# A two-layer recurrent and attention trunk: weight splits by halves, one copy of the small vectors, a later broadcast, and an earlier root table

## The chip, the cores and the metric

The kernel runs on one core of one Trainium2 chip. The metric is the device time of one execution in microseconds (us); of several runs the median is given. TensorE (PE in the profile, PEld for its weight loads) multiplies, VectorE (DVE), ScalarE (ACT) and GpSimd (POOL) work element by element, and SyncE (SP) issues nearly all DMA transfers. Each engine works through its own list of instructions in order and waits on semaphores where an instruction needs another engine's or a DMA's result.

## The reference

The input x has 1024 rows of 1024 numbers, in float32. Two layers follow each other; each has a token mixer and a feed-forward block, both with a residual add and an RMS norm ahead of them, and a last RMS norm ends the program. This is what is computed, cut to what matters here:

```python
def rms_norm(x, g):
    return x * lax.rsqrt(jnp.mean(x * x, axis=-1, keepdims=True) + 1e-6) * g

for layer in range(2):
    hn = rms_norm(h, mix_norm[layer])
    mixed = rg_lru_block(hn, ...) if layer == 0 else stick_breaking_attention(hn, ...)
    h = h + mixed
    h = h + swiglu_ffn(rms_norm(h, ffn_norm[layer]), ffn_w_in[layer], ffn_w_out[layer])
return rms_norm(h, final_norm)
```

The mixer of layer 0 projects the normed input to a recurrent branch and a gate branch (`lru_w_in`), runs a causal convolution of width 4 over the recurrent branch, forms two gates with block-diagonal weights (`lru_gate_w`), and scans `h = a * h + b` over the rows, where `a` depends on a softplus of `lru_lambda`. That of layer 1 is an attention with 16 heads of 64.

## The kernel before

**Tiling.** Activations are kept transposed, as `[d][n]` tiles of 128 features by 512 rows (n is 0 or 1). To keep float32 accuracy, each operand of a product is split into a rounded part and a rest (`xh` and `xl`, `whi` and `wlo`), and `mm3` (L140) issues three matmuls for each pair: L141 whi with xh, L142 whi with xl, L143 wlo with xh. A weight tile of 1024 x 128 is loaded as `raw`, ACT casts it to `whi` (L120), and POOL subtracts for `wlo` (L124). `raw` has three buffers; `whi` and `wlo` come from a ring of six, so a new weight pair waits until the matmuls have read the pair three before it.

**First phase (L251 to L359).** The order on every engine is the written one. SP loads x in eight parts, two weight tiles and nine small vectors (into `vraw`, L285). `group(n, d)` (L298) transposes four blocks on TensorE; ACT writes `xh` (L304), DVE writes a copy `hc` (L308) that SP stores to DRAM (L310), and then `xl` (L309). `project` (L247) makes 24 matmuls for one column tile and one half n. `square_rows` (L312) sums squares on ACT; `row_factors` (L316) turns them into the norm's factors through `rstd` (L174); `broadcast_r` (L185) spreads the factors over all partitions, with four transposes into PSUM on TensorE and a copy to `rbc[n]` on DVE (L196). The norm's factor is applied after the product: `stage_a` multiplies the result by `rbc[n]` (L444). At the end of this phase the broadcast of the second half's factors stands between the first and the second half of the last 24 matmuls (L357 to L359). The small vectors are transposed to columns `vc` at L345, with a matmul that waits for all of `vraw`'s transfers itself.

**Second phase (L362 to L518).** Only TensorE keeps the written order; the other engines' instructions are ordered by the framework's scheduler. A chain of some 45 tiny DVE instructions (L371 to L405) works out the softplus and the convolution's bias from `vc`: seven of them are L379, followed by L382 to L385. Then column tiles are projected, convolved (L446, L448), gated and scanned, in the order "A0 A1 B0 A2 G0 A3 ...". A0 and A1 use the two results of the first phase; B0 is the first projection of the gate branch, with PSUM from a pool (`psB`, L364) that takes over the banks of the first phase's pool `sps`. G0 needs the first gate weights, `rawg` (L415), which pass through the same cast and subtraction (L120, L124).

**The middle** is the two feed-forward blocks (seven products in place of eight by a Strassen-like scheme) and the attention; none of its lines is edited, except that `rstd` is used there too.

**The end (`finish`, L1215).** The last two feature tiles are finished in pieces: all four blocks of rows of n = 0, blocks 0 and 1 of n = 1, and blocks 2 and 3 of n = 1. `last` (L1220) makes the product, adds it to the residual (L1230), squares it (L1231), adds to the sum of squares (L1232) and applies the gain. `stats` (L198) sums over features by TensorE, and `rstd` makes the factors: a root on ACT (L178) and five small DVE instructions (L179 to L183). `turn` (L1235) transposes back (L1244), scales each block by its factor on ACT (L1246, odd blocks) or DVE (L1248), and SP stores it (L1249).

Of the kernel before, what the change touches and what calls it, by code (L numbers as in the profile page):

```python
# [8 lines left out]
F32 = mybir.dt.float32  # L9
F32R = mybir.dt.float32r  # L10
# [3 lines left out]
ALU = mybir.AluOpType  # L14
PSUM = bass.MemoryType.PSUM

P = 128
S = 1024
D = 1024
ND = D // P  # L20
# [13 lines left out]
def trunk(  # L34
# [22 lines left out]
    nc = tc.nc  # L57
    f32 = lambda t: t.bitcast(F32)
# [29 lines left out]
    wpool = [ring]  # L88


    ident = cp.tile([P, P], F32, name="ident")
    make_identity(nc, ident)
    ones = cp.tile([P, 1], F32, name="ones")
    nc.gpsimd.memset(ones, 1.0)
    vc = cp.tile([P, P], F32, name="vc")
# [11 lines left out]
    rcol = cp.tile([P, NT], F32, name="rcol")  # L107
# [9 lines left out]
    def split(raw, pool=None, tag="w", bufs=None, lo_eng=None, parts=1):  # L117
        pool = pool or wpool[0]
        hi = pool.tile([P, D], F32R, tag=tag, name="whi", bufs=bufs)
        nc.scalar.copy(hi, raw)  # L120
        lo = pool.tile([P, D], F32R, tag=tag, name="wlo", bufs=bufs)
        for i in range(parts):
            c = slice(i * D // parts, (i + 1) * D // parts)
            (lo_eng or nc.gpsimd).tensor_sub(lo[:, c], raw[:, c], f32(hi)[:, c])  # L124
        return hi, lo
# [48 lines left out]
    def rstd(dst, ms):  # L174
        n = dst.shape[-1]
        sq = cp.tile([P, max(n, 4)], F32, tag="rs_s", name="rs_s", bufs=2)[:, 0:n]
        t = cp.tile([P, max(n, 4)], F32, tag="rs_t", name="rs_t", bufs=2)[:, 0:n]
        nc.scalar.sqrt(sq, ms)  # L178
        nc.vector.reciprocal(sq, sq)  # L179
        nc.vector.tensor_mul(t, sq, sq)  # L180
        nc.vector.tensor_mul(t, t, ms)
        nc.vector.tensor_scalar(t, t, -0.5, 1.5, op0=ALU.mult, op1=ALU.add)
        nc.vector.tensor_mul(dst, sq, t)  # L183

    def broadcast_r(ps_pool, tag, n):  # L185
        ps = ps_pool.tile([P, NB], F32, tag=tag, name="rb_ps")
# [55 lines left out]
    half = lambda t, n: t[:, n * NB : (n + 1) * NB]  # L242
# [4 lines left out]
    def project(ps, w, n, ks=range(ND)):  # L247
        for k in ks:
            mm3(half(ps, n), w[0][:, k], w[1][:, k], xh[k][n], xl[k][n], k == 0, k == ND - 1)

    with ExitStack() as st, tc.manual_schedule(engines={E.PE, E.Activation, E.DVE, E.Pool, E.SP}):  # L251
        sp = st.enter_context(tc.tile_pool(name="sp", bufs=1))
        sps = st.enter_context(tc.tile_pool(name="sps", bufs=4, space=PSUM))
        vraw = sp.tile([P, P], F32, name="vraw")
        vmix = sp.tile([P, P], F32, name="vmix")
        g0 = sp.tile([P, ND], F32, name="g0")
        nc.scalar.dma_start(vmix[0:ND, :], mix_norm[0:1].rearrange("a (b c) -> (a b) c", c=P))
        xt = [sp.tile([P, 4, D], F32, name=f"xt{n}") for n in range(NH)]
        aw = []

        def load_x(n, g):
            cs = slice(g * 2 * P, (g + 1) * 2 * P)
            nc.sync.dma_start(
                xt[n][:, :, cs], x[0, n * NB : (n + 1) * NB, cs].rearrange("(i p) c -> p i c", p=P)
            )

        for g in range(3):
            load_x(0, g)
        aw.append(load_raw(cols(w_in, D), (ND,)))
        load_x(0, 3)  # L270
        aw.append(load_raw(cols(w_in, D + P), (ND,)))
        load_x(1, 0)
        load_x(1, 1)
        for base, src in (
            (V_MIX, mix_norm.rearrange("a (b c) -> (a b) c", c=P)),
            (V_FFN, ffn_norm.rearrange("a (b c) -> (a b) c", c=P)),
            (V_FIN, final_norm.rearrange("(b c) -> b c", c=P)),
            (V_BIN, lru_b_in.rearrange("a (b c) -> (a b) c", c=P)),
            (V_CW, lru_conv_w.rearrange("a k (b c) -> (a k b) c", c=P)),
            (V_CB, lru_conv_b.rearrange("a (b c) -> (a b) c", c=P)),  # L280
            (V_GB, lru_gate_b.rearrange("a g (b c) -> (a g b) c", c=P)),
            (V_LAM, lru_lambda.rearrange("a (b c) -> (a b) c", c=P)),
            (V_BO, lru_b_out.rearrange("a (b c) -> (a b) c", c=P)),
        ):
            nc.sync.dma_start(vraw[base : base + src.shape[0], :], src)  # L285
        load_x(1, 2)
        load_x(1, 3)
        ssum = sp.tile([P, NT], F32, name="ssum")
        ms = sp.tile([P, NT], F32, name="ms0")
        junk = sp.tile([P, D], F32, name="junk")  # L290
        pst = lambda name: sps.tile([P, NB], F32, tag="tp", name=name)
        k3 = lambda t: t.rearrange("p (k c) -> p k c", k=ND)

        ps = pst("vps0")
        nc.tensor.transpose(ps[:, 0:ND], vmix[0:ND, :], ident[0:ND, 0:ND])
        nc.vector.tensor_copy(g0, ps[:, 0:ND])

        def group(n, d):  # L298
            ps = pst("tp")
            for i in range(4):  # L300
                nc.tensor.transpose(ps[:, i * P : (i + 1) * P], xt[n][:, i, d * P : (d + 1) * P], ident)
            hc = sp.tile([P, NB], F32, tag="hc", name="hc", bufs=8)
            g = g0[:, d : d + 1]
            nc.scalar.activation(xh[d][n], ps, AF.Copy, scale=g)  # L304
            if d % 4 == 3:
                nc.scalar.copy(hc, ps)
            else:
                nc.vector.tensor_copy(hc, ps)  # L308
            nc.vector.scalar_tensor_tensor(xl[d][n], ps, g, f32(xh[d][n]), op0=ALU.mult, op1=ALU.subtract)  # L309
            nc.sync.dma_start(hd[d][n], hc)  # L310

        def square_rows(n, i):  # L312
            b = 4 * n + i
            nc.scalar.activation(junk, xt[n][:, i, :], AF.Square, accum_out=ssum[:, b : b + 1])

        def row_factors(n):  # L316
            nn = slice(4 * n, 4 * n + 4)
            nc.vector.tensor_scalar(ms[:, nn], ssum[:, nn], 1.0 / D, EPS, op0=ALU.mult, op1=ALU.add)
            rstd(rcol[:, nn], ms[:, nn])

        def wsplit(i):
            hi, lo = split(aw[i])
            aw[i] = (k3(hi), k3(lo))

        pa = [psl[0].tile([P, S], F32, tag="a", name="a_ps") for _ in range(2)]
        for d in range(6):
            group(0, d)
        wsplit(0)
        for d in (6, 7):
            group(0, d)  # L330
        wsplit(1)
        for i in range(4):
            square_rows(0, i)
        project(pa[0], aw[0], 0)
        group(1, 0)
        group(1, 1)
        row_factors(0)
        project(pa[1], aw[1], 0, range(4))
        group(1, 2)
        group(1, 3)  # L340
        project(pa[1], aw[1], 0, range(4, ND))
        group(1, 4)
        group(1, 5)
        ps = pst("vps")
        nc.tensor.transpose(ps[:, 0:P], vraw, ident)  # L345
        nc.vector.tensor_copy(vc, ps[:, 0:P])
        square_rows(1, 0)
        square_rows(1, 1)
        project(pa[0], aw[0], 1, range(4))
        group(1, 6)  # L350
        group(1, 7)
        square_rows(1, 2)
        square_rows(1, 3)
        broadcast_r(sps, "tp", 0)
        project(pa[0], aw[0], 1, range(4, ND))
        row_factors(1)
        project(pa[1], aw[1], 1, range(4))  # L357
        broadcast_r(sps, "tp", 1)
        project(pa[1], aw[1], 1, range(4, ND))  # L359


    with ExitStack() as st:  # L362
# [45 lines left out]
        ys = [lp.tile([P, S], F32, name=f"y{e}") for e in range(ND)]  # L408
# [188 lines left out]
    def mix_out_ffn_in(h, mix, bias, layer, gnext, ob):  # L597
# [124 lines left out]
        with tc.manual_schedule(engines={E.PE, E.Activation, E.DVE, E.Pool}):  # L722
# [484 lines left out]
            if final:  # L1207
                finish(h, nw, R, pp, (*GT, *UT))
# [6 lines left out]
    def finish(h, w, R, pp, rows):  # L1215
        ys = {}
# [18 lines left out]
        def turn(n, i0, i1, hf):  # L1235
            cs = slice(hf * NB, (hf + 1) * NB)
            for i in range(i0, i1):
                b = 4 * n + i
                if hf == 0:
                    ys[b] = rp.tile([P, D], F32, tag="raw", name="y") if b < 3 else rows[b - 3]  # L1240
                ps = pp.tile([P, NB], F32, tag="p", name="e_ps")
                for j in (1, 2, 3, 0):
                    d = 4 * hf + j
                    nc.tensor.transpose(ps[:, j * P : (j + 1) * P], h[d][n][:, i * P : (i + 1) * P], ident)  # L1244
                if i % 2:
                    nc.scalar.activation(ys[b][:, cs], ps, AF.Copy, scale=rcol[:, b : b + 1])  # L1246
                else:
                    nc.vector.tensor_scalar_mul(ys[b][:, cs], ps, rcol[:, b : b + 1])  # L1248
                nc.sync.dma_start(out[0, b * P : (b + 1) * P, cs], ys[b][:, cs])  # L1249

        first, mid, end = (0, 0, 4), (1, 0, 2), (1, 2, 4)
        for piece in (first, mid):
            for x in range(2):
# [39 lines left out]
    with ExitStack() as st:  # L1293
# [249 lines left out]
        with tc.manual_schedule(engines={E.PE, E.Activation, E.DVE, E.Pool, E.SP}):  # L1543
# [20 lines left out]
            c = 0  # L1564
# [69 lines left out]
```

## Time and profile before

| | us |
|---|---|
| median of 3 runs | 2195.74 |
| lowest and highest of them | 2195.57 and 2196.19 |
| time of the profiled execution | 2195.37 |
| its span, first to last instruction | 2193.6 |
| TensorE busy in the span | 2167.9 |
| VectorE busy | 1711.4 |
| ScalarE busy | 1155.4 |
| GpSimd busy | 315.7 |

In the profile's rows a line of the timeline has the start in us from the start of the span, the duration in us, the engine, the line of the kernel, the operation, output and inputs with shapes, a count where equal instructions follow each other, and in brackets how long the engine had been idle before it and what ended that. A row of the waits has the engine and line that waited, what it waited for, the us in total, how many times, and the longest.

### The profile page before, as it was taken

What the parts mean: (1) busy time and instruction counts of PE and PEld (TensorE: products, weight loads), DVE (VectorE), ACT (ScalarE), POOL (GpSimd) and SP (SyncE); (2) the same over time, 40 slices, a digit from 0 to 9 for tenths busy, and PEclk for the clock granted to TensorE, in tenths of its full rate; (3) what the DMA queues carried; (4) which work ended last, traced back from release to release, by engine and by line L of the source; (5) the groups of instructions that cost most, each with busy time, mean ns of one, the idle gap of its engine ahead of it and who ended that gap; (6) DMA issues with size and microseconds to landing.
All of it is one profiled execution on the core that took longest, in us unless ns stands there. A gap on an engine that the chain in (4) does not pass through costs nothing.

```text
span 2193.6 us, 28494 instructions
## 1 busy us (share of the span) xinstructions
PE 2167.9 (99%) x10120; PEld 1803.3 (82%) x10120; DVE 1711.4 (78%) x2383; ACT 1155.4 (53%) x2031; POOL 315.7 (14%) x443
## 2 busy tenths in 40 slices
PE   8999999999999999999999999999999999999998
PEld 6888888888888888888888888878888888888887
DVE  6887778667777887887888888876876777788886
ACT  5567435334444544556666666753543444454556
POOL 2222020000000000004444444531000000000002
PEclk9999999999999999999999999999999999999999
DMA  7111412334444764434333333551133444467442
GB/s 232 49 48 39 135 39 64 110 125 152 141 145 138 250 221 129 148 117 104 89 106 90 94 98 105 173 169 54 48 115 116 149 146 143 144 228 236 137 153 87
DMA packets 297677, 277.71 MB, mean 127 GB/s; under 512 B 15288, under 2 KB 214080, under 8 KB 297536
## 3 DMA queue, kind: packets, MB, share of 16 engines
q1 hardware_dynamic: 297520, 275.90, 40.6%
q8 instruction: 79, 1.29, 0.2%
q14 instruction: 62, 0.51, 0.1%
q10 hardware_dynamic: 16, 0.00, 0.0%
HBM read 175.71 MB, written 74.97 MB: 114 GB/s over the span
## 4 chain that ended last, share of the span: by engine, by line
PE 95%; DVE 2%; ACT 1%; DMA 1%; SPq 0%; issue 0%; DVEq 0%; ACTq 0%
PE p_ps L143 18%; PE p_ps L141 18%; PE p_ps L142 18%; PE qk_ps L143 4%; PE qk_ps L141 4%; PE qk_ps L142 4%; PE wt_ps L1465 3%; PE ob_ps L141 2%; PE ob_ps L142 2%; PE ob_ps L143 2%; PE a_ps L141 2%; PE a_ps L142 2%; PE a_ps L143 2%; PE z_ps L1427 2%; PE z_ps L1428 2%; PE av_ps L1487 2%
## 5 line engine op out<-in xcount | busy, mean ns | idle before, releaser
L1452 POOL TENSOR_TENSOR w<-w,F 128x128 f32<-128x128 f32 (+1 forms) x192 | 192.5, 1002 | 268.3 <-DVE F L1449 164.6
L141 PE MATMUL p_ps<-vh,wch 128*128 128x512 f32 x524 | 204.2, 390 | 0.0
L143 PE MATMUL p_ps<-vh,wal 128*128 128x512 f32 x524 | 204.1, 389 | 0.1
L143 PE MATMUL p_ps<-vh,wbl 128*128 128x512 f32 x524 | 204.1, 390 | 0.0
L143 PE MATMUL p_ps<-vh,wcl 128*128 128x512 f32 x524 | 204.1, 390 | 0.0
L141 PE MATMUL p_ps<-vh,wbh 128*128 128x512 f32 x524 | 204.1, 390 | 0.0
L142 PE MATMUL p_ps<-vl,wch 128*128 128x512 f32 x524 | 203.9, 389 | 0.0
L142 PE MATMUL p_ps<-vl,wbh 128*128 128x512 f32 x524 | 203.9, 389 | 0.0
L141 PE MATMUL p_ps<-vh,wah 128*128 128x512 f32 x524 | 203.9, 389 | 0.0
L142 PE MATMUL p_ps<-vl,wah 128*128 128x512 f32 x524 | 203.8, 389 | 0.0
L668 ACT CAST wbh<-sb 128x1024 fp32r<-128x1024 f32 (+2 forms) x69 | 69.6, 1009 | 193.1 <-DVE sb L652 193.1
L1474 ACT CAST th<-wt_ps 128x512 fp32r<-128x512 f32 x192 | 92.6, 482 | 126.3 <-PE wt_ps L1465 125.8
L212 POOL TENSOR_TENSOR acc<-acc,rbc 128x512 f32<-128x512 f32 x30 | 41.6, 1386 | 771.9 <-ACT rbc L211 771.9
L1475 DVE TENSOR_TENSOR tl<-wt_ps,th 128x512 fp32r<-128x512 f32 x192 | 105.6, 550 | 48.9 <-ACT th L1474 46.9
L141 PE MATMUL qk_ps<-vh,whi 128*128 128x512 f32 x264 | 118.1, 447 | 0.0
L1449 DVE TENSOR_TENSOR_SCAN F<-F,unit 128x128 f32<-128x128 f32 (+3 forms) x128 | 115.4, 902 | 2.8 <-ACT F L1445 2.6
L143 PEld LDWEIGHTS p_ps<-vh,wbl 128*128 128x128 f32 x524 | 98.4, 188 | 21.4 <-DVE wbl L672 0.8
L143 PEld LDWEIGHTS p_ps<-vh,wal 128*128 128x128 f32 x524 | 98.3, 188 | 21.4 <-DVE wal L663 1.0
L143 PEld LDWEIGHTS p_ps<-vh,wcl 128*128 128x128 f32 x524 | 98.3, 188 | 21.1 <-DVE wcl L682 0.6
L141 PEld LDWEIGHTS p_ps<-vh,wch 128*128 128x128 f32 x524 | 98.4, 188 | 20.8 <-ACT tb L1057 0.5
L141 PEld LDWEIGHTS p_ps<-vh,wah 128*128 128x128 f32 x524 | 98.4, 188 | 20.4
L142 PEld LDWEIGHTS p_ps<-vl,wah 128*128 128x128 f32 x524 | 98.4, 188 | 20.4
(341 smaller groups left out, 5858.3 us busy)
## 6 DMA issues: line engine op xcount, KB each, us to landing
raw<-in_ffn_w_in SPq DMA_DIRECT2D x88, 512.0 KB, 4.0
vl<-pd SPq DMA_DIRECT2D x128, 256.0 KB, 3.6
pd<-U SPq DMA_DIRECT2D x90, 256.0 KB, 2.3
kk<-two SPq DMA_DIRECT2D x64, 256.0 KB, 4.2
raw<-in_ffn_w_out SPq DMA_DIRECT2D x56, 256.0 KB, 3.9
raw<-in_attn_w_qkv SPq DMA_DIRECT2D x24, 512.0 KB, 4.1
raw<-in_lru_w_in SPq DMA_DIRECT2D x16, 512.0 KB, 4.0
q<-two SPq DMA_DIRECT2D x64, 128.0 KB, 2.3
```

Source lines behind the costliest of these rows:

```text
L141: nc.tensor.matmul(ps, lhsT=wh, rhs=mh, start=first, stop=False, **kw)
L142: nc.tensor.matmul(ps, lhsT=wh, rhs=ml, start=False, stop=False, **kw)
L143: nc.tensor.matmul(ps, lhsT=wl, rhs=mh, start=False, stop=last, **kw)
L668: nc.scalar.copy(self.full(self.wb), self.full(self.sb))
L1427: nc.tensor.matmul(ps[:, 0 : c1 - c0], lhsT=lhsT, rhs=KK[q][hx][:, 0, c0:c1], start=True, stop=False)
L1428: nc.tensor.matmul(ps[:, 0 : c1 - c0], lhsT=lhsT, rhs=KK[q][hx][:, 1, c0:c1], start=False, stop=True)
L1449: nc.vector.tensor_tensor_scan(rev, rev, unit[:, NB - n :][:, ::-1], first, op0=ALU.mult, op1=ALU.add)
L1452: nc.gpsimd.tensor_mul(wt, wt, F[:, 1 : n + 1])
L1465: nc.tensor.transpose(tp[:, c : c + P], W[q, hx, j, kb // 4][:, (kb % 4) * P : (kb % 4 + 1) * P], ident)
L1474: nc.scalar.copy(th[:, q0:], tp[:, q0:])
L1475: nc.vector.tensor_sub(tl[:, q0:], tp[:, q0:], f32(th)[:, q0:])
L1487: nc.tensor.matmul(ps[:, q0:], lhsT=VV[q][:, kb, hx], rhs=tl[:, q0:], start=False, stop=last)
```

## The change

`rstd` forms the same Newton step with two fused instructions in place of three, so it has four DVE instructions where there were five. In the first phase a weight tile's cast and subtraction are issued by halves of 512 columns; the small vectors are copied on POOL to a new tile `vall`, and TensorE transposes that tile, after the last group of n = 1, where it transposed `vraw` before that half's first products; the broadcast of the second factors stands behind the whole of the last 24 matmuls, where it stood in their middle. At the end a root of a constant is issued on ACT before `finish` begins its pieces, which brings the table load for roots there, and the last block's store is issued by ACT where SP issued it.

```diff
@@ rstd
         nc.vector.tensor_mul(t, sq, sq)
-        nc.vector.tensor_mul(t, t, ms)
-        nc.vector.tensor_scalar(t, t, -0.5, 1.5, op0=ALU.mult, op1=ALU.add)
-        nc.vector.tensor_mul(dst, sq, t)
+        nc.vector.scalar_tensor_tensor(t, t, -0.5, ms, op0=ALU.mult, op1=ALU.mult)
+        nc.vector.scalar_tensor_tensor(dst, t, 1.5, sq, op0=ALU.add, op1=ALU.mult)
@@ first phase
         def wsplit(i):
-            hi, lo = split(aw[i])
+            hi, lo = (wpool[0].tile([P, D], F32R, tag="w", name=x) for x in ("whi", "wlo"))
+            for c in range(2):
+                nc.scalar.copy(half(hi, c), half(aw[i], c))
+                nc.gpsimd.tensor_sub(half(lo, c), half(aw[i], c), f32(half(hi, c)))
             aw[i] = (k3(hi), k3(lo))
...
         group(1, 4)
         group(1, 5)
-        ps = pst("vps")
-        nc.tensor.transpose(ps[:, 0:P], vraw, ident)
-        nc.vector.tensor_copy(vc, ps[:, 0:P])
         square_rows(1, 0)
         square_rows(1, 1)
         project(pa[0], aw[0], 1, range(4))
         group(1, 6)
         group(1, 7)
+        vall = sp.tile([P, P], F32, name="vall")
+        nc.gpsimd.tensor_copy(vall, vraw)
+        ps = pst("vps")
+        nc.tensor.transpose(ps[:, 0:P], vall, ident)
+        nc.vector.tensor_copy(vc, ps[:, 0:P])
         square_rows(1, 2)
         square_rows(1, 3)
         broadcast_r(sps, "tp", 0)
         project(pa[0], aw[0], 1, range(4, ND))
         row_factors(1)
-        project(pa[1], aw[1], 1, range(4))
+        project(pa[1], aw[1], 1)
         broadcast_r(sps, "tp", 1)
-        project(pa[1], aw[1], 1, range(4, ND))
@@ finish
-                nc.sync.dma_start(out[0, b * P : (b + 1) * P, cs], ys[b][:, cs])
+                queue = nc.scalar if (n, i, hf) == (1, 3, 1) else nc.sync
+                queue.dma_start(out[0, b * P : (b + 1) * P, cs], ys[b][:, cs])
...
+        nc.scalar.sqrt(rcol[:, 0:1], ones)
         first, mid, end = (0, 0, 4), (1, 0, 2), (1, 2, 4)
```

In the built program the edits also move instructions of the second phase, where the scheduler orders ACT, DVE, POOL and SP anew. On DVE the copy to `rbc[1]` (L196) stands behind both first-half products of L444 and behind L379 to L385; before, it stood behind one of the products and ahead of L377 and L379. On ACT the cast of `rawg` (L120) stands directly behind the root of the second factors (L178), where a convolution's first step (L446) stood between them. On SP the second of the two `rawg` loads stands behind the stores of the last two `hc` tiles. On TensorE the four transposes of the second broadcast stand directly ahead of B0's first matmul, and that matmul waits, before as after, for the copy to `rbc[1]`, which empties the PSUM bank. From the gate stage on, the order of every engine is as before, up to the end.

## The prediction

> **What bounds the kernel now.** The page's first part gives the bound, and the waits of TensorE say where it stands idle.
>
> ```profile
> PE 2167.9 (99%) x10120; PEld 1803.3 (82%) x10120; DVE 1711.4 (78%) x2383; ACT 1155.4 (53%) x2031; POOL 315.7 (14%) x443
> ```
>
> TensorE is busy for 99% of the span, so nearly all of the time is matmuls that this change leaves alone. What can move are the few waits. Those of the first 60 us that bear on the edits, from the table of waits (us in total, times, longest):
>
> ```profile
> PE rb_ps L189 <- DVE rcol L183: 1.8, 1, 1.8
> PE a_ps L143 <- POOL wlo L124: 1.3, 1, 1.3
> PE vps L345 <- issue: 1.0, 1, 1.0
> PE a_ps L142 <- DVE xl L309: 0.6, 1, 0.6
> ```
>
> The change goes at the first three: 4.1 us. Which of them is worth anything depends on what ends last behind them, so I read TensorE's timeline from the fourth wait on:
>
> ```profile
> 35.92 0.50 PE L142 MATMUL a_ps<-xl,whi 128*128 128x512 f32 x1 [0.65 <-DVE xl L309]
> ...
> 39.66 0.39 PE L143 MATMUL a_ps<-xh,wlo 128*128 128x512 f32 x1
> 41.86 1.16 PE L189 MATMUL rb_ps<-ident,rcol 128*128 128x128 f32 x8 [1.81 <-DVE rcol L183]
> 42.77 0.48 PE L141 MATMUL a_ps<-xh,whi 128*128 128x512 f32 x1
> ...
> 45.59 0.39 PE L141 MATMUL a_ps<-xh,whi 128*128 128x512 f32 x1
> ```
>
> The matmul at 45.59 is the first of B0. Matmuls in steady state start 0.227 us apart (twelve between 42.77 and 45.59, with the first slower).
>
> **The change, part by part.**
>
> *Weights by halves, and the small vectors' copy: worth nothing.* Both bring TensorE earlier to the wait that ends at 35.92, by up to 1.3 + 1.0 us, and it would wait there longer. That `xl` comes from DVE, which waits for ACT, and ACT's chain is this:
>
> ```profile
> 31.80 1.05 ACT L120 CAST whi<-raw 128x1024 fp32r<-128x1024 f32 x1 [1.52 <-DMA raw<-in_lru_w_in]
> ...
> 37.67 1.04 ACT L120 CAST whi<-raw 128x1024 fp32r<-128x1024 f32 x1
> 38.61 0.20 ACT L178 ACTIVATE rs_s<-ms 128x4 f32<-128x4 f32 x1
> 44.92 1.24 ACT L446 ACTIVATE rec<-u,cb,vc 128x1024 f32<-128x1024 f32 x1 [6.12 <-DVE u L444]
> 46.07 1.03 ACT L120 CAST whi<-rawg 128x1024 fp32r<-128x1024 f32 x1
> ```
>
> ACT stood idle for 1.52 us until a weight's DMA landed at 31.80, and did the last `xh` behind it. The transfers before that run without a pause (DMA share 1.01):
>
> ```profile
> 20.00:32.00 12.00, 10.96 (x61) 9.09 (x60) 8.08 (x18) 6.79 (x12) 0.00 (x0) 1.00 1.01 353
> ```
>
> No edit moves fewer bytes there, so 35.92 stays. Were the DMA ahead, the two edits would give 2.3 us less the 0.65 us of that wait's length; I take 0 between 0 and -1.7. The split's extra instructions (two casts and two subtractions, some 0.1 us each) lie in ACT's 1.52 us. POOL's copy to `vall` has no row of its kind; the nearest are POOL's 2.37 us for 128x1024, below, eight times the size, and nothing. I take 0.3 us; POOL is idle there, so it costs 0.
>
> *The second factors behind the products: this decides.* TensorE no longer waits at 39.89 for `rcol`: it goes on with twelve matmuls to 39.89 + 12 x 0.227 = 42.61, then makes the broadcast (42.77 - 41.86 = 0.91) to 43.52. The factors are there by then (below, 41.6). So 1.81 us go, and B0 could begin 2.1 us sooner. But B0's first matmul waits for the copy to `rbc[1]`. In the kernel before, twelve matmuls lay between broadcast and B0, and hid the copy; now nothing does. And DVE makes this copy in its own order, which now is: factors, 17 tiny instructions, first product of L444, two tiny ones, seven L379, L382, L383, L384, second product of L444 (tile 1), L385, then the copy. The rows for these, from DVE's timeline:
>
> ```profile
> 39.05 2.12 DVE L180 TENSOR_TENSOR rs_t<-rs_s 128x4 f32<-128x4 f32 x1
> 41.20 0.16 DVE L181 TENSOR_TENSOR rs_t<-rs_t,ms 128x4 f32<-128x4 f32 x1
> 41.40 0.17 DVE L182 TENSOR_SCALAR rs_t<-rs_t 128x4 f32<-128x4 f32 x1
> ...
> 42.86 0.69 DVE L444 TENSOR_TENSOR u<-a_ps,rbc 128x512 f32<-128x512 f32 x1
> 43.46 0.68 DVE L196 COPY rbc<-rb_ps 128x512 f32<-128x512 f32 x1
> ...
> 44.80 1.37 DVE L379 SCALAR_TENSOR_TENSOR pq<-pq,gq 128x8 f32<-128x8 f32 x7
> 46.20 0.17 DVE L382 SCALAR_TENSOR_TENSOR pq<-pq,two 128x8 f32<-128x8 f32 x1
> ...
> 61.08 2.36 DVE L390 SCALAR_TENSOR_TENSOR pq<-kq,pq 128x8 f32<-128x8 f32 x1
> ```
>
> Factors end at 41.40 + 0.16 = 41.6. The tiny ones between 41.40 and 42.86 came every 0.08 us, so the first product starts at 42.7 and yields at 43.3 (0.60, as 42.86 to 43.46). Two tiny ones: 43.45. Then L379, one each 0.2 us (1.40 / 7), to 44.85; L382 to L384 0.2 each: 45.4; second product, 46.0; copy 46.1 to 46.8. That would put B0 at 46.8, were DVE undisturbed.
>
> It is not. Two rows above stand out: L180 and L390, on 4 and 8 columns, took 2.12 and 2.36 us, against 0.16 for their like. POOL's timeline says why:
>
> ```profile
> 38.78 2.37 POOL L124 TENSOR_TENSOR wlo<-raw,whi 128x1024 fp32r<-128x1024 f32 x1 [3.46 <-ACT whi L120]
> 47.18 3.30 POOL L124 TENSOR_TENSOR wlo<-rawg,whi 128x1024 fp32r<-128x1024 f32 x1 [6.03 <-ACT whi L120]
> 60.79 2.63 POOL L124 TENSOR_TENSOR wlo<-raw,whi 128x1024 fp32r<-128x1024 f32 x1 [10.31 <-ACT whi L120]
> ```
>
> L180 ended at 41.17, 0.02 us after POOL's subtraction; L390 at 63.44, also 0.02 after POOL's. A DVE instruction with two tensor inputs in SBUF stands still while POOL subtracts. Before, `rawg`'s subtraction came at 47.18, when the copy was long done. Now ACT casts `rawg` directly behind the root at 38.61; the cast waits only for the ring's buffer, which the second-last matmul of the 24 reads last: 42.61 - 2 x 0.227 + 0.39 = 42.55. POOL starts 1.11 us behind a cast's start (46.07 to 47.18): at 43.7, amid the L379, and holds to 46.1. Two of the seven are done by then; the third ends at 46.1, four more at 46.95, L382 to L384 at 47.5, the product yields at 48.1, and the copy runs to 48.85. **B0 starts at 48.9, against 45.59: +3.3 us.** TensorE stands idle from 43.7 on, 5.2 us. `rawg` itself must have landed by 42.55:
>
> ```profile
> DMA to landing us min/median/max: 2.9/5.6/5.8
> ```
>
> Its second load is now issued behind the last two `hc` stores,
>
> ```profile
> 35.23 0.82 SPq L310 DMA_DIRECT2D hd<-hc  x2
> ```
>
> so at 36.1; with 5.8 us it lands at 41.9. Later, POOL's hold would only move against the same chain. The undisturbed sum (46.8, +1.2) is the other end.
>
> *The clock.* Such a pause has a second price. Two stretches of the attention, busy, granted clock:
>
> ```profile
> 1454.16:1457.57 3.41, 1.24 (x9) 1.06 (x10) 3.30 (x5) 0.71 (x3) 2.08 (x2) 1.00 0.00 0
> 1457.57:1460.99 3.42, 3.42 (x16) 3.12 (x15) 2.49 (x5) 2.38 (x5) 0.11 (x1) 0.50 0.00 0
> ```
>
> After 3.41 us with TensorE busy for 1.24, the clock was 0.50 for the next 3.41. If these windows keep their phase (1454.16 less 413 windows of 3.4133 is 44.46), the one from 44.46 to 47.87 is wholly idle, and that to 51.28 runs at half clock: 51.28 - 48.9 = 2.4 us, half lost: **+1.2** (0.7 to 2.4 for other phases; 0 if the clock stays). From there TensorE runs on without a wait as before, all other engines being less late than it, so both sums reach the end.
>
> *The factors with one instruction less.* 0.2 us each. In the middle, TensorE's other work covers it: 0. At the end it counts, with the next.
>
> *Root table sooner.*
>
> ```profile
> 2175.18 0.51 ACT L1233 ACTIVATE hh<-hh,vc 128x256 f32<-128x256 f32 x1
> 2175.71 1.28 ACT L178 ACT_TABLE_LOAD   x1
> 2177.00 0.21 ACT L178 ACTIVATE rs_s<-ms 128x4 f32<-128x4 f32 x1
> ```
> ```profile
> 2178.05 0.16 DVE L183 TENSOR_TENSOR rcol<-rs_s,rs_t 128x4 f32<-128x4 f32 x1
> 2178.32 1.41 DVE L1248 TENSOR_SCALAR y<-e_ps,rcol 128x512 f32<-128x512 f32 x2
> ...
> 2182.21 0.41 DVE L1230 TENSOR_TENSOR hh<-o_ps,hh 128x256 f32<-128x256 f32 x1
> ```
> ```profile
> 2179.05 1.53 PE L1244 MATMUL e_ps<-ident,hh 128*128 128x128 f32 x12 [0.73 <-ACT y L1246]
> ...
> 2181.72 0.28 PE L143 MATMUL o_ps<-vh,wrl 128*128 128x256 f32 x1
> ```
>
> The load of 1.28 us lies on the chain between the sums and the root; now it falls in ACT's idle time before L1231, where a delay of 0.1 us hits nothing. With the shorter factors the first `y` come 1.46 us sooner. The next piece then hangs on TensorE, which loses its 0.73 us wait and some 0.15 of restart: its product ends 0.88 sooner, at 2181.12, so L1230 starts at 2181.15, -1.06. Two more factor chains follow, 0.2 each: **-1.46** at the last block. The Trainium skill's page "ScalarE: Activation LUTs" (section "What ACT_TABLE_LOAD costs") gives a drain of 1380 ns beside the load, 2.66 us for a switch; by that the sum would be 1.4 us lower, 2197.3. The trace of before shows ACT's neighbours close to the load on both sides (2175.18 + 0.51 ahead, 2177.00 behind), so I give that no chance of its own.
>
> *The last store by ACT.* It need not wait for SP's earlier issues (some 0.4 us each), so it could start 0.5 sooner. But the DMA engines are full then:
>
> ```profile
> 2190.00:2192.20 2.20, 0.00 (x0) 0.00 (x0) 0.00 (x0) 0.00 (x0) 0.00 (x0) 0.83 0.99 368
> ```
>
> 256 KB at 368 GB/s are 0.7 us, and four such blocks queue up; the order of issue changes nothing. I take 0, between -0.5 and +0.2.
>
> **The sum**: 3.3 + 1.2 - 1.46 = +3.0 on the profiled execution's 2195.37: 2198.4. The median of the runs stands 0.37 above, so I predict 2198.7, 0.14% slower: inside the 0.2% (4.4 us) that a measurement of this kernel can tell from no change.
>
> **Rivals.**
>
> *DVE undisturbed*: POOL does not hold DVE at L379, or the clock stays whole. With +1.2 for B0, an idle stretch of 3.1 us and, by its busy share in the window, a half-clock window of 1.7: 2.9 - 1.5, 2197.2. With the hold but full clock, 2197.6. The rows L180 and L390 speak against the first. "TensorE: Matmul & The Clock Gate" (the Trainium skill, section "What's actually happening") puts the half clock after at least one idle window of about 3.4 us; by that 3.1 us would go free, 2195.5. The row of 1454.16, with 1.24 us busy, disagrees.
>
> *It does what it says*: the copy comes right behind the broadcast, B0 at 44.5, -1.1, and -1.46 at the end: 2193.2. For it: all data are there. Against it: DVE's order.
>
> *Other half-clock windows*: the attention's two windows depend on how its pauses fall into windows of 3.41 us; the shift of 3 to 4.5 us can free one (1.7 less: 2197.0) or add one (1.7 more: 2200.4). **This is the slower case**: it decides from 1.4 us over my sum, as does a second half-clock window behind B0's pause (2.4 in place of 1.2).
>
> **How the numbers follow.** My forecast has 0.50, its own range 2197.8 to 2200.0 (clock price 0.7 to 2.4, less 0.4 for DVE's start). DVE undisturbed, full clock or a freed window: 0.26, 2195.5 to 2197.6. It does what it says: 0.09, of which 0.03 end below 2191.35 with two freed windows. Slower by over 0.2%, above 2200.1: 0.15. Same holds the rest, 0.82. Leaving out half of the third case and the upper part of the fourth gives 2194.0 to 2200.8.
>
> **What would show it.** Right: the wait of `rb_ps` for `rcol` gone; a wait of about 5 us ahead of B0's first L141, put down to `rbc`; an L379 of over 2 us beside POOL's subtraction of `rawg`; a granted clock of 0.50 behind it; no table load after 2170, and the first `y` 1.5 us sooner against the end. Wrong: B0 before 45.6, L379 at 1.4 us for seven, or a wait at the fourth row above that is gone.

## The result, and the profile after

| | before | after |
|---|---|---|
| median of 15 runs each, us | 2195.56 | 2200.09 |
| lowest and highest | 2195.06, 2196.19 | 2198.88, 2202.11 |
| profiled execution, us | 2195.37 | 2200.59 |
| its span, us | 2193.6 | 2198.7 |

The change made the kernel 4.5 us slower: a ratio of 1.0021, with a 95% interval of 1.0014 to 1.0028. The forecast was 2198.7, so it is 1.4 us short. The runs of after also lie further apart than those of before (3.2 against 1.1 us).

Busy time and the waits of TensorE in after (engine and line, what it waited for, us in total, times, longest), two views, stand next:

```profile
PE 2170.2 (99%) x10120; PEld 1805.0 (82%) x10120; DVE 1710.8 (78%) x2374; ACT 1155.8 (53%) x2034; POOL 316.8 (14%) x446
```
```profile
PE a_ps L141 <- DVE rbc L195: 5.4, 1, 5.4
...
PE a_ps L142 <- DVE xl L308: 0.9, 1, 0.9
```

The wait of `rb_ps` for the factors (1.8 us), that for `wlo` (1.3) and that of `vps` (1.0) are gone, as the change meant. One wait of 5.4 us ahead of B0 has come in their place. TensorE's own busy time rose by 2.3 us with the same number of matmuls, so some of them ran slower.

The timeline of after around that wait:

```profile
32.99 1.04 ACT L120 CAST whi<-raw 128x1024 fp32r<-128x1024 f32 x1 [1.53 <-DMA raw<-in_lru_w_in]
...
37.10 0.50 PE L142 MATMUL a_ps<-xl,whi 128*128 128x512 f32 x1 [0.89 <-DVE xl L308]
...
43.79 1.05 PE L188 MATMUL rb_ps<-ident,rcol 128*128 128x128 f32 x8
43.81 1.04 ACT L120 CAST whi<-rawg 128x1024 fp32r<-128x1024 f32 x1 [3.82 <-PE a_ps L142]
...
44.79 3.51 DVE L384 SCALAR_TENSOR_TENSOR pq<-pq,gq 128x8 f32<-128x8 f32 x7
44.93 2.34 POOL L124 TENSOR_TENSOR wlo<-rawg,whi 128x1024 fp32r<-128x1024 f32 x1 [2.57 <-ACT whi L120]
...
48.86 0.64 DVE L449 TENSOR_TENSOR u<-a_ps,rbc 128x512 f32<-128x512 f32 x1
...
49.49 0.68 DVE L195 COPY rbc<-rb_ps 128x512 f32<-128x512 f32 x1
...
50.23 0.79 PE L141 MATMUL a_ps<-xh,whi 128*128 128x512 f32 x1 [5.38 <-DVE rbc L195]
```

The broadcast runs at 43.79 without a wait. Its copy on DVE comes only at 49.49, behind seven tiny instructions (before's L379 is L384 here) that took 3.51 us in place of 1.37, beside POOL's subtraction from 44.93 to 47.27. B0 starts at 50.23. I count from the wait for the last `xl`, which is at 35.92 before and at 37.10 here: B0 came 9.67 us behind it before, and 13.13 now, **+3.46**.

The same stretch, cut where the granted clock can change (each row has a stretch, its length, busy us of PE, PEld, DVE, ACT and POOL with the number of instructions, then granted clock, DMA share and GB/s):

```profile
43.44:46.85 3.41, 1.41 (x11) 1.14 (x9) 3.38 (x13) 1.04 (x1) 1.92 (x1) 1.00 0.54 156
46.85:50.26 3.41, 0.04 (x1) 0.04 (x1) 3.14 (x14) 0.00 (x0) 0.42 (x1) 0.50 0.43 119
50.26:53.68 3.42, 3.42 (x8) 2.74 (x9) 3.32 (x10) 2.37 (x2) 0.00 (x0) 0.50 0.13 37
53.68:57.09 3.41, 3.41 (x16) 2.79 (x16) 3.41 (x5) 0.00 (x0) 0.00 (x0) 1.00 0.03 5
```

From 50.23 to 53.68 TensorE worked at half clock and lost half of 3.45 us, **+1.72**. At full clock 16 matmul rows fit into a window, here 8.

The end of after on ACT, and one row of before for it:

```profile
2174.29 1.28 ACT L1259 ACT_TABLE_LOAD   x1
...
2181.75 0.51 ACT L1238 ACTIVATE hh<-hh,vc 128x256 f32<-128x256 f32 x1
2182.28 0.20 ACT L178 ACTIVATE rs_s<-ms 128x4 f32<-128x4 f32 x1
...
2192.80 1.27 ACT L1251 ACTIVATE U<-e_ps,rcol 128x512 f32<-128x512 f32 x2 [0.88 <-DVE rcol L182]
```
```profile
2187.74 1.27 ACT L1246 ACTIVATE U<-e_ps,rcol 128x512 f32<-128x512 f32 x2 [1.08 <-DVE rcol L183]
```

The table load is off the chain: the root follows the gain (L1238) at once. That gain is 2181.75 - 2175.18 = 6.57 us later than in before, the last block's scaling only 2192.80 - 2187.74 = 5.06, so the end gave back **1.51**. The load itself delays nothing where it now is: the first gain behind it is 2176.34 - 2169.76 = 6.58 us later than in before, as late as the last one.

Together: 3.46 + 1.72 - 1.51 = 3.7 of the 5.1 us between the spans. 1.18 lie ahead of the last `xl` (37.10 against 35.92), and so ahead of the moved broadcast. They are there already when ACT has waited for a weight's DMA: the cast behind that wait starts at 32.99 here and at 31.80 before, after 1.53 and 1.52 us of idling. Whether the early edits make this landing late is tested below. The rest, 0.2, is in the middle.

### The profile page after: what moved, and what is told of

Same layout as the page of the kernel before. It is cut to its first block, busy times and chain, and to the rows that moved or that the text cites. A ratio compares the mean times of both kernels' runs of the same rounds, so it can differ in the third digit from the quotient of the medians.

```text
span 2198.7 us, 28493 instructions
## 1 busy us (share of the span) xinstructions
PE 2170.2 (99%) x10120; PEld 1805.0 (82%) x10120; DVE 1710.8 (78%) x2374; ACT 1155.8 (53%) x2034; POOL 316.8 (14%) x446
## 4 chain that ended last, share of the span: by engine, by line
PE 94%; DVE 3%; ACT 1%; DMA 1%; SPq 1%; issue 0%; DVEq 0%; ACTq 0%
PE p_ps L141 18%; PE p_ps L143 18%; PE p_ps L142 18%; PE qk_ps L143 4%; PE qk_ps L141 4%; PE qk_ps L142 4%; PE wt_ps L1474 3%; PE ob_ps L142 2%; PE ob_ps L141 2%; PE ob_ps L143 2%; PE a_ps L141 2%; PE a_ps L142 2%; PE a_ps L143 2%; PE z_ps L1436 2%; PE z_ps L1437 2%; PE av_ps L1496 2%
## 5 line engine op out<-in xcount | busy, mean ns | idle before, releaser
L141 PEld LDWEIGHTS p_ps<-vh,wbh 128*128 128x128 f32 x524 | 98.4, 188 | 20.6 <-ACT ta L1062 0.2
```

The source lines that it names most:

```text
L141: nc.tensor.matmul(ps, lhsT=wh, rhs=mh, start=first, stop=False, **kw)
```

## The experiments

The theory: the whole loss is the broadcast's place, through DVE's order, POOL's hold on DVE and the half clock; the end gains 1.5; everything else is nothing. The rivals: the first phase's early edits delay its start (the 1.18), the place itself costs (the bank that B0 needs), the order on DVE alone costs and POOL has no part, or the end's gain is lost in the stores. Each kernel was timed beside before on the same chip, in three groups on three chips; kernels of different groups are compared by how far each stands from its own before. The intervals reach some 2 us to each side, so where a difference is near that, the runs' own ends and the traces are read beside it.

| kernel | median us | before there | ratio, 95% interval |
|---|---|---|---|
| after, broadcast back in the middle | 2194.00 | 2195.67 | 0.9991, 0.9982 to 1.0000 |
| before, broadcast behind | 2200.95 | 2195.67 | 1.0027, 1.0016 to 1.0037 |
| after, copy by ACT | 2193.18 | 2195.67 | 0.9989, 0.9980 to 0.9997 |
| after, POOL held back | 2198.18 | 2195.67 | 1.0009, 1.0000 to 1.0018 |
| before, factors and root only | 2193.97 | 2195.85 | 0.9991, 0.9983 to 1.0000 |
| before, halves and `vall` only | 2196.34 | 2195.85 | 1.0002, 0.9993 to 1.0011 |
| after, last store by SP | 2200.67 | 2195.85 | 1.0022, 1.0013 to 1.0031 |
| after again | 2200.00 | 2195.85 | 1.0019, 1.0010 to 1.0028 |
| after, TensorE kept busy | 2198.33 | 2195.76 | 1.0012, 1.0003 to 1.0021 |
| after, broadcast 6 matmuls ahead, copy by ACT | 2192.61 | 2195.76 | 0.9985, 0.9976 to 0.9994 |

**Which part: one alone, one undone.** The broadcast put back:

```diff
-        project(pa[1], aw[1], 1)
+        project(pa[1], aw[1], 1, range(4))
         broadcast_r(sps, "tp", 1)
+        project(pa[1], aw[1], 1, range(4, ND))
```

> The changed kernel with the second broadcast put back between the two halves of the last 24 matmuls; all other edits stay. If the place of the broadcast is the whole loss (the wait of 5.4 us ahead of B0 and the half clock behind it), both go, the end keeps its 1.5 us, and the time is 2195.6 - 1.5 = 2194.1 us. If the 1.2 us by which the first phase ran late in the changed kernel's profile belong to the other early edits (halves, copy of the small vectors), the time is 2195.3. If the gain of the end is not there in the time, 2195.6 or more.

It took 2194.00, 1.67 less than before: the loss is gone, and the gain of the end is left.

The same move the other way round, in the kernel before, as its only edit:

```diff
-        project(pa[1], aw[1], 1, range(4))
+        project(pa[1], aw[1], 1)
         broadcast_r(sps, "tp", 1)
-        project(pa[1], aw[1], 1, range(4, ND))
```

> The kernel before with only the second broadcast moved behind the last 24 matmuls. If this is the whole loss: B0 3.5 us later and 1.7 us of half clock, 2195.6 + 5.2 = 2200.8 us, more than the whole change. If the first phase's other edits carry a part of it, 1.2 us or so less than that against the whole change: about 2199.6 with the pause shorter. If the place costs nothing, 2195.6.

It took 2200.95, +5.3 us. Its timeline and its windows:

```profile
35.48 0.50 PE L142 MATMUL a_ps<-xl,whi 128*128 128x512 f32 x1 [0.17 <-DVE xl L309]
...
48.83 0.80 PE L141 MATMUL a_ps<-xh,whi 128*128 128x512 f32 x1 [5.58 <-DVE rbc L196]
```
```profile
45.05:48.47 3.42, 0.00 (x0) 0.00 (x0) 3.11 (x13) 0.00 (x0) 0.63 (x1) 1.00 0.36 97
48.47:51.88 3.41, 3.05 (x7) 2.47 (x8) 3.31 (x10) 2.34 (x2) 0.00 (x0) 0.50 0.20 59
```

The wait and the half clock are there without any other edit. B0 is 13.35 behind the last `xl`, 3.68 more than in before, and works at half clock for 3.05 us, which loses 1.5: together 5.2 of the 5.3.

The early edits without the broadcast, in the kernel before (the halves and the later transpose of `vall`, as in the change's own diff):

```diff
-            hi, lo = split(aw[i])
+            hi, lo = (wpool[0].tile([P, D], F32R, tag="w", name=x) for x in ("whi", "wlo"))
+            for c in range(2):
+                nc.scalar.copy(half(hi, c), half(aw[i], c))
+                nc.gpsimd.tensor_sub(half(lo, c), half(aw[i], c), f32(half(hi, c)))
...
-        nc.tensor.transpose(ps[:, 0:P], vraw, ident)
...
+        nc.gpsimd.tensor_copy(vall, vraw)
...
+        nc.tensor.transpose(ps[:, 0:P], vall, ident)
```

> The kernel before with only the weights split by halves, the small vectors copied by POOL and transposed later (the first phase's edits without the broadcast). The prediction puts these at nothing: 2195.7 us, with the wait of a_ps for xl longer than 0.65 and ending at the same time after the last x arrives. If they start the first phase 1.2 us late, as the changed kernel's profile has it, 2196.9. If the waits that they remove were on the path, up to 1.7 less: 2194.0.

2196.34, which can't be told from before. Its waits show why they bring nothing:

```profile
PE rb_ps L189 <- DVE cb L406: 1.9, 1, 1.9
...
PE a_ps L142 <- DVE xl L309: 1.1, 2, 0.9
```

The waits for `wlo` and `vps` are gone and the one for `xl` is longer, as the prediction had it (0.65 before, 0.9 here).

And the end's edits alone in the kernel before, without the store:

```diff
-        nc.vector.tensor_mul(t, t, ms)
-        nc.vector.tensor_scalar(t, t, -0.5, 1.5, op0=ALU.mult, op1=ALU.add)
-        nc.vector.tensor_mul(dst, sq, t)
+        nc.vector.scalar_tensor_tensor(t, t, -0.5, ms, op0=ALU.mult, op1=ALU.mult)
+        nc.vector.scalar_tensor_tensor(dst, t, 1.5, sq, op0=ALU.add, op1=ALU.mult)
...
+        nc.scalar.sqrt(rcol[:, 0:1], ones)
```

> The kernel before with only the shorter factors and the early root (no other edit). If the end's 1.46 us are real and all of the gain, 2195.7 - 1.5 = 2194.2 us, and the kernel with the broadcast put back (2194.0) holds nothing beside it. If the stores at the end, which queue up for the DMA engines, absorb the gain, 2195.7. If the first phase's early edits carry a gain of their own, this kernel stays above 2194.5.

2193.97, 1.9 less than before. The interval just reaches 1, but ten of the eleven runs lie below the fastest of before's 33, and in its profile the last block's scaling follows the last gain 1.49 us sooner than in before: the end's gain is real, and of the size foreseen.

The store back on SP:

```diff
-                queue = nc.scalar if (n, i, hf) == (1, 3, 1) else nc.sync
+                queue = nc.sync
```

> The changed kernel with the last block's store issued by SP again. If the order of issue changes nothing at the end, the same as the changed kernel, 2200.1 us. If ACT's issue gained, up to 0.5 more; if it cost, 0.2 less.

2200.67 against 2200.00 for after on the same chip, with intervals that overlap: no difference that these runs show. From the last block's scaling to the end of the span it is 5.9 us with either queue (2198.7 - 2192.80 in after, 2199.2 - 2193.31 here).

The kernel after once more, unchanged:

> The changed kernel itself once more, on the same chip as its parts. If the parts add up (broadcast alone +5.3, end alone -1.5, the rest nothing), 2195.7 + 3.8 = 2199.5 us; the first measurement had 2200.1. The runs should lie some 3 us apart where those of the kernel before lie 1 to 2 apart, if the half-clock window behind B0's pause falls differently in each run; the start of the first phase in its profile should be another one than in the first profile if that was the run's and not the kernel's.

2200.00, +4.15. The parts (5.3 - 1.9 + 0.5, the last inside its uncertainty) give 3.9. The start of its first phase differs from that of the first profile, by the same wait for the last `xl`:

```profile
35.56 0.50 PE L142 MATMUL a_ps<-xl,whi 128*128 128x512 f32 x1 [0.88 <-DVE xl L308]
...
48.56 0.79 PE L141 MATMUL a_ps<-xh,whi 128*128 128x512 f32 x1 [5.21 <-DVE rbc L195]
```

35.56, where the first profile of the same kernel had 37.10. In the profiles of the experiments it lies between 35.09 and 36.66, and the kernel with 36.66 has no edit but the factors' ahead of it. The nine profiles with the early edits (35.09 to 37.10) and the three without them (35.48 to 36.66) overlap. So the 1.18 us are that execution's and not the change's, and this rival falls. B0 stands 13.00 behind it, against 13.13 in the first profile, and two windows at half clock follow each other here too; B0 starts near the end of the first:

```profile
46.03:49.45 3.42, 0.89 (x2) 0.80 (x3) 3.22 (x14) 0.18 (x1) 0.00 (x0) 0.50 0.57 153
49.45:52.86 3.41, 3.41 (x9) 2.64 (x9) 3.31 (x8) 2.19 (x2) 0.00 (x0) 0.50 0.01 2
```

**Why B0 waits: order or hold.** POOL's subtraction of `rawg` kept back, while DVE's order stays the same, instruction by instruction:

```diff
-            hi, lo = split(raw)
+            hi = wpool[0].tile([P, D], F32R, tag="w", name="whi")
+            nc.scalar.copy(hi, raw)
+            lo = wpool[0].tile([P, D], F32R, tag="w", name="wlo")
+            if b == 0:
+                nc.gpsimd.tensor_copy(lo[:, 0:1], rbc[1][:, 0:1])
+            nc.gpsimd.tensor_sub(lo, raw, f32(hi))
```

> The changed kernel with POOL's subtraction of rawg kept until rbc[1] is copied (POOL first copies one column of rbc[1] into the tile that it then overwrites). DVE's order is the same, instruction by instruction. If POOL's subtraction holds DVE, the seven L384 take 1.4 us instead of 3.5, B0 comes 2.1 us sooner, the half clock costs 1.1 instead of 1.7: 2200.1 - 2.7 = 2197.4 us. If the slow L384 have another cause and only the order counts, 2200.1.

```profile
35.94 0.50 PE L142 MATMUL a_ps<-xl,whi 128*128 128x512 f32 x1 [0.89 <-DVE xl L308]
...
43.62 1.37 DVE L384 SCALAR_TENSOR_TENSOR pq<-pq,gq 128x8 f32<-128x8 f32 x7
...
46.18 0.68 DVE L195 COPY rbc<-rb_ps 128x512 f32<-128x512 f32 x1
...
46.92 0.50 PE L141 MATMUL a_ps<-xh,whi 128*128 128x512 f32 x1 [3.22 <-DVE rbc L195]
...
47.26 2.39 POOL L429 TENSOR_TENSOR wlo<-rawg,whi 128x1024 fp32r<-128x1024 f32 x1
...
47.50 2.17 DVE L392 TENSOR_SCALAR kq<-gq 128x8 f32<-128x8 f32 x1
```
```profile
47.89:51.30 3.41, 3.41 (x9) 2.65 (x9) 3.31 (x7) 1.97 (x2) 1.76 (x1) 0.50 0.07 15
```

The same seven instructions take 1.37 us when POOL does not subtract beside them, against 3.51. The hold is shown, and it is worth 2.1 us: B0 is 46.92 - 35.94 = 10.98 behind the last `xl`, 1.31 more than before. That 1.31 is what the broadcast's new place costs through the order on DVE alone. By the Trainium skill's page "SBUF — State Buffer" (section "Who interferes with whom") a DVE instruction with two SBUF inputs contends with a GpSimd instruction that reads SBUF; this pair of rows agrees.

The hold is not confined to such instructions in this trace: L392, with one tensor input in SBUF, stood beside POOL's late subtraction for 2.17 us and ended 0.02 us after it (49.67 and 49.65). Nor does it strike every one: in the last kernel below a reciprocal (L390) took 0.20 us beside a subtraction.

The median stands 2.5 above its before, where after's stood 4.15 and 4.53: it fell by 1.6 to 2.0, not 2.7. In its profile the half clock covers 47.89 to 51.30, all of it matmuls, 1.7 us, where I had 1.1. Its runs lie 3.1 us apart. What is left of the difference stays open.

The copy moved to ACT, so that neither order nor hold reaches it:

```diff
-        nc.vector.tensor_copy(rbc[n], ps)
+        (nc.scalar.copy if n and tag == "tp" else nc.vector.tensor_copy)(rbc[n], ps)
```

> The changed kernel with the copy to rbc[1] made by ACT in place of DVE; ACT does it behind its cast of rawg, and the place of the broadcast stays. If the loss is DVE's order and POOL's hold on it, B0 comes right behind the broadcast and the copy, some 1 us after the last product's end instead of 5.4, no half clock follows: 4.7 + 1.7 less than the changed kernel's 2200.1, so 2193.7 us. If the loss lies in the place itself (the bank that B0 needs, the broadcast on TensorE's path), the time stays at about 2200.

```profile
36.07 0.50 PE L142 MATMUL a_ps<-xl,whi 128*128 128x512 f32 x1 [0.89 <-DVE xl L308]
...
43.76 3.59 DVE L384 SCALAR_TENSOR_TENSOR pq<-pq,gq 128x8 f32<-128x8 f32 x7
43.89 0.58 ACT L195 COPY rbc<-rb_ps 128x512 f32<-128x512 f32 x1
43.94 2.38 POOL L124 TENSOR_TENSOR wlo<-rawg,whi 128x1024 fp32r<-128x1024 f32 x1 [2.62 <-ACT whi L120]
...
44.53 0.50 PE L141 MATMUL a_ps<-xh,whi 128*128 128x512 f32 x1 [0.68 <-ACT rbc L195]
```

DVE is held just as long (3.59), and it costs nothing, because nothing that TensorE waits for stands behind it. It took 2193.18, 2.5 less than before: the place of the broadcast is no loss in itself, which ends that rival. B0 comes 44.53 - 36.07 = 8.46 behind the last `xl`, 1.21 sooner than before; the prediction's rival "it does what it says" had 1.1.

**What the half clock costs.** Twenty matmuls fill TensorE's wait; nobody reads their result:

```diff
         broadcast_r(sps, "tp", 1)
+        ps = pst("fill")
+        for i in range(20):
+            nc.tensor.matmul(ps, lhsT=xh[1][0][:, 0:P], rhs=xh[0][0], start=True, stop=True)
```

> The changed kernel with 20 extra matmuls on TensorE between the second broadcast and B0, whose result nobody reads; they take 20 x 0.227 = 4.5 us and lie wholly inside the wait of 5.2 to 5.4 us for rbc[1]. If that wait is of its own worth 3.4 us and the half clock behind it the rest, B0 starts at the same place and the half clock (1.5 to 2.8 us in the four profiles with the pause) goes: 2200.0 - 2.0 = 2198.0 us. If the half clock costs nothing at the end of the program, 2200.0; if the extra matmuls are in the way, more.

```profile
35.67 0.51 PE L142 MATMUL a_ps<-xl,whi 128*128 128x512 f32 x1 [0.88 <-DVE xl L308]
...
43.21 4.81 PE L367 MATMUL fill<-xh,xh 128*128 128x512 f32 x20
...
48.14 0.68 DVE L195 COPY rbc<-rb_ps 128x512 f32<-128x512 f32 x1
...
48.98 0.47 PE L141 MATMUL a_ps<-xh,whi 128*128 128x512 f32 x1 [0.95 <-DVE gq L394]
```
```profile
47.40:52.00 4.60, 3.65 (x16) 2.73 (x15) 4.50 (x13) 2.38 (x2) 0.00 (x0) 1.00 0.38 112
```

B0 starts about where it did (48.98 - 35.67 = 13.31 behind the last `xl`, against 13.13 and 13.00). Its row names L394, a tiny instruction behind the copy; the copy of `rbc[1]` ends at 48.82. The clock stays at 1.00, and the median stands 2.57 above its before, where after's stood 4.15 and 4.53. So 1.6 to 2.0 of after's loss are the clock's, and the later start is a cost by itself.

**A version from the explanation.** The broadcast behind 18 of the 24 matmuls, when the factors are nearly there, and the copy by ACT, by the same edit as above:

```diff
-        project(pa[1], aw[1], 1)
+        project(pa[1], aw[1], 1, range(6))
         broadcast_r(sps, "tp", 1)
+        project(pa[1], aw[1], 1, range(6, ND))
```

> The changed kernel with the broadcast six matmuls before the end of the last 24 (behind 18 of them) and the copy to rbc[1] made by ACT, ahead of its cast of rawg. If the explanation holds, the wait for the factors shrinks from 1.6 us to 0.2, the six matmuls behind the broadcast (1.4 us) hide the copy, and nothing is left of the 0.7 us that B0 waits where the whole broadcast stands behind the products: 2195.7 - 1.4 - 1.5 = 2192.8 us, 0.4 less than with the copy by ACT alone. If ACT's extra copy delays the cast of rawg or G0, 2193.2 or more.

```profile
42.14 1.13 PE L188 MATMUL rb_ps<-ident,rcol 128*128 128x128 f32 x8 [0.32 <-DVE az L377]
...
43.30 0.59 ACT L195 COPY rbc<-rb_ps 128x512 f32<-128x512 f32 x1 [4.09 <-PE rb_ps L188]
...
44.49 0.39 PE L141 MATMUL a_ps<-xh,whi 128*128 128x512 f32 x1
```

The wait for the factors is 0.32 (its row names the tiny instruction behind them), the copy lies under six matmuls, and B0 (44.49) waits for nothing. 2192.61 is 3.15 us less than before, and so 7.3 less than after, which stood 4.15 above its own.

## Why the prediction was nearly right, and where it was short

- **Halves, `vall` and the last store by ACT: 0.** Right, as far as the runs tell: the first two alone gave +0.5, inside the interval, and the store by ACT stands 0.7 below that by SP, with intervals that overlap.
- **B0 waits for the copy, +3.3.** Right in mechanism and size: +3.46 and +3.33 in the two profiles of after. Its lower end without POOL's hold, +1.2, was 1.31 in the kernel that holds POOL back.
- **The clock, +1.2.** The mechanism was right, the size was not. This is the term that was mis-sized: 1.2 in the sum, 1.5 to 2.8 in the profiles. It rested on "if these windows keep their phase": I placed a window at 44.46 to 47.87 by counting from one in the attention. The phase differs from execution to execution. In four profiles with the same wait, B0 ran at half clock from its start for 3.45 us (after), 52.86 - 48.56 = 4.30 (after again), 51.88 - 48.83 = 3.05 (before with the broadcast behind) and 54.74 - 49.07 = 5.67 (after with SP's store), of which half is lost: 1.7, 2.2, 1.5 and 2.8, on the mean 2.1. The page "TensorE: Matmul & The Clock Gate" of the Trainium skill (section "What's actually happening") says that the window runs free and does not reset when a kernel starts. The profiles agree: counted from the span's start, the edges near B0 are 46.85, 46.03, 48.47 and 47.91 in these four.
- **The end, -1.46.** Right: -1.51 in the profile, -1.9 in the median of the kernel with these edits alone. The load's neighbours stand close to it again (the gain ahead of it ends at 2174.29, the root of the constant starts at 2175.58, 0.01 us behind its end), so the drain that the prediction quoted from the Trainium skill's page "ScalarE: Activation LUTs" (section "What ACT_TABLE_LOAD costs") does not show here either. One sign was put wrongly: "no table load after 2170". The load is at 2174.29 of after's span, which is ahead of `finish`'s pieces, as meant.
- **The sum.** 3.4 + 2.1 - 1.5 = 4.0, where measurements gave 4.5 and 4.15. What is left, 0.2 to 0.5, I can't assign: the start of the first phase scatters by 1 to 2 us from execution to execution, and the attention has one or two half-clock windows (from 1430.27 and 1457.57 in before, from 1463.38 in after). The first median, 2200.09, lies just above the range that the prediction gave its own case (2197.8 to 2200.0), at the border of the one that it called slower.
- **The rivals.** "DVE undisturbed" falls by the row of 3.51. "It does what it says" falls for this kernel, and became true when ACT made the copy. The slower case named a second half-clock window behind B0's pause: three of the four profiles just listed have two half-clock windows in a row. In after the first of them lies inside the pause and costs nothing; in after again and in after with SP's store B0 works in both, for 4.30 and 5.67 us. So its mechanism is there, and the forecast should have held part of it.

## What to carry to other kernels

A transfer or reduction that is moved behind a block of matmuls to save a wait takes along its consumer: before moving it, read which matmul waits for the copy of its result and what the copying engine does first in its own order. A wait of several microseconds on TensorE can cost more than the delay that it brings, because the clock can go down behind it: here a wait of 5.4 us put B0 back by 3.4 and lost 2 more at half clock, and one of 3.2 lost 1.7, while waits of 0.68 (copy by ACT) and 1.59 us (broadcast back in the middle) lost none. Two executions can differ by 1 to 2 us at the start, so count from a common event (here the last `xl`) and not from the span's start.

## What the runs showed of the clock

In these twelve profiles the granted clock changes only at the edges of windows of 3.41 us (in after it is 0.50 from 46.85 to 53.68, two of them). Which clock the next window gets goes, in the main, by how busy TensorE was in this one. After a window at full clock it went down behind 1.41 us busy of 3.41 (after, 43.44, above), and stayed up behind this one of before, with 1.53:

```profile
10.32:13.73 3.41, 1.53 (x10) 1.13 (x10) 3.41 (x6) 3.03 (x5) 1.80 (x1) 1.00 1.14 321
13.73:17.14 3.41, 2.79 (x12) 2.32 (x13) 1.49 (x3) 3.38 (x6) 2.71 (x2) 1.00 0.45 135
```

Yet before with the broadcast behind went down after 1.64 of 3.41 in its window from 7.51, so the edge is not a sharp one, or busy time is not quite what counts. After a window at half clock, more is needed to go up again: 2.26 us busy were not enough in after with SP's store, where B0 starts within that window,

```profile
49.07 0.80 PE L141 MATMUL a_ps<-xh,whi 128*128 128x512 f32 x1 [5.37 <-DVE rbc L195]
```
```profile
44.50:47.91 3.41, 0.00 (x0) 0.00 (x0) 3.14 (x10) 0.00 (x0) 1.62 (x1) 1.00 0.09 24
47.91:51.33 3.42, 2.26 (x5) 1.82 (x6) 3.32 (x12) 1.55 (x2) 0.00 (x0) 0.50 0.46 137
51.33:54.74 3.41, 3.41 (x9) 2.64 (x8) 3.41 (x5) 0.82 (x1) 0.00 (x0) 0.50 0.00 0
54.74:58.15 3.41, 3.41 (x16) 2.79 (x15) 3.41 (x7) 0.63 (x1) 0.00 (x0) 1.00 0.02 5
```

while 3.05 us were, in the window from 48.47 of before with the broadcast behind. That a busy microsecond at half clock counts half would fit these two, but it was only argued, and not all rows bear it out: after again came back behind 2.84 us (its window from 1435.26), which would count 1.42, where 1.41 at full clock lost the clock in after. I had not expected it: a pause that ended 1.16 us into a window (49.07, above) cost the rest of that window and the whole next one. The Trainium skill's page "TensorE: Matmul & The Clock Gate" (section "What's actually happening") puts the half clock behind one idle window or more. The rows differ, with 0.50 behind a window in which TensorE was busy for 1.41 of 3.41 us.
